# Second mixer of a fused three-layer block: low halves of weights and modulation products taken off GpSimd and put on VectorE in whole tiles

## The chip, the cores and the metric

The kernel runs on one core of one Trainium2 chip. The metric is the device time of one execution in microseconds (us), the median of several runs. The engines are named as in the profile: PE is TensorE (matmuls), PEld its weight loads, DVE is VectorE, ACT is ScalarE, POOL is GpSimd, and SP is SyncE, which issues the DMAs.

## The reference

Three layers are computed in turn over 256 tokens of width 1024. The first is a block with two sparse attentions, the second a block with differential attention (`diff_mixer`), the third a block with a gated delta rule and an axial attention. The change lies in the second layer's mixer, whose reference is:

```
ada = c_act @ ada_w[l] + ada_b[l]
sh1, sc1, g1, sh2, sc2, g2 = jnp.split(ada, 6, axis=-1)
h = modulate(x, sh1, sc1)
q, k, v = jnp.split(h @ w_in, 3, axis=-1)           # 8 heads, each with two 64-wide maps
logits = jnp.einsum('bqhmd,bshmd->bhmqs', qq, k) * scale + bias
p = masked_softmax(logits, dist >= 0)
pd = p[:, :, 0] - lam_full * p[:, :, 1]
o = jnp.einsum('bhqs,bshe->bqhe', pd.astype(v.dtype), v)
o = rms_norm(o, subln) * (1.0 - lambda_init)
y = o @ w_out
```

The modulation vectors (`ada`, six of 1024 values for each of the first two layers) come from a matrix of 1024 x 6144 times one vector.

## The kernel before

**Weights in two halves.** Every weight tile is 128x1024 in float32 (512 KB). It is loaded into a buffer `raw`, ACT rounds it to `hi` (line 347), and the remainder `lo = raw - hi` is a subtraction of two tiles in SBUF (line 352), on DVE or on POOL. Each product is then three matmuls: hi x hi, lo x hi, hi x lo (lines 387 to 389).

**Modulation vectors.** A vector is eight tiles of `ada_w`, each multiplied by the activated conditioning row (`cact`, repeated in all partitions) and summed along its row. `ada_dot` does this for one tile in one of two ways: one DVE instruction that multiplies and sums (line 478, printed as `CUSTOM_DVE_ANT_0` and followed by a short read of the accumulator), or two products of half tiles on POOL (line 461) and a sum on ACT (line 474).

**The second mixer** (`mix1`) works through a list: eight tiles of the value projection (v0 to v7), then q and k of each of the eight heads, one tile of 24 matmuls each, then the output projection. `weave` takes this list one tile at a time and between pieces advances the chains: the eight heads (`queue1`, `head1`), the modulation vectors (1, 3) and (1, 4) (`weave_ada`), and a small preparation for the third layer (`meta_prep`). In this stage the order of instructions on ACT, DVE and POOL is that of the code (`MAN[1]` is `ADG`); the order on PE is left to the scheduler, which sets it when the kernel is built. DMAs are issued by SP in the order of the code, into a ring of seven `raw` buffers, so a load goes out when the tile seven loads earlier has been used.

**Whose low halves.** `SHARE1 = 6`: of the tiles that `weave` prepares here, the first six get a whole `lo` on DVE, the other 20 half on DVE and half on POOL:

```
if share is not None and n > share:
    self.cast_lo(x, nc.vector, 0)
    self.cast_lo(x, nc.gpsimd, 1)
else:
    self.cast_lo(x, nc.vector)
```

**One head** (`head1`): its scores are four matmuls (line 401) into PSUM tiles `y` and `c`; DVE adds the bias and takes the row minimum (line 1625, four instructions); ACT takes the exponentials with row sums (`exps`, line 1658); DVE inverts the sums and scales two of them (lines 1633 and 1634, `drs`); POOL multiplies the second map by them (line 1636, two instructions); DVE combines the two maps (line 1639, two instructions); PE transposes the result (line 1643, `tr<-p_first,se`); ACT copies it (line 1645); PE multiplies it with the values (line 392, into `d`). After every second head `pair1` normalises: squares on ACT (line 1670, `dof`), scalars on DVE (1673), a power on POOL (1674), the product on DVE (1676), transposes on PE (1680), and the split into halves on ACT and DVE (1682, 1684). ACT also copies each q and k out of PSUM (line 1586, `f<-y`); there are two PSUM banks for them.

The eight heads are numbered 0 to 7 in the text.

Of the kernel before, what the change touches and what calls it, by code (L numbers as in the profile page):

```python
# [29 lines left out]
ADA0 = 16  # L30
# [1 line left out]
ADA1 = 17  # L32
ORDER1 = """v0 v1 v2 v3 v4 v5 v6 v7 q0 k0 q1 k1 q2 k2 q3 k3 q4 k4 q5 k5 q6 k6 q7 k7"""
MORE1 = 2
SHARE1 = 6
SHARE0 = None
SHARE2 = 8
MAN = ['A', 'ADG', 'AD', 'ADG', 'P']
# [228 lines left out]
class Kern:  # L267
# [768 lines left out]
    def layer0(self, stop):  # L1036
        nc, ph = self.nc, self.ph
        st = self.st = SimpleNamespace(tok=False, cmp=0, sel=0, lat=False, pc=False, scored=0)
        self.F, self.part, self.oh, self.L0 = {}, {}, None, None
        self.blk = self.T(self.acts, (128, 16, 64), "ol")  # L1040
        nc.gpsimd.memset(self.blk, 0.0)
        self.blkw = self.T(self.acts, (128, 16, 128), "oh", F32R)
        self.tok = self.T(ph, (128, 2, 416), "tok")
        self.hs = self.T(ph, (128, 256), "isc", bufs=3)
        work = []
        for n in ORDER0.split():
            f = (lambda wh, wl, i=int(n[-1]): self.tok0(i, wh, wl)) if n[:3] == "tok" else \
                (lambda wh, wl, n=n[4], i=int(n[5]): self.cmp0(n, i, wh, wl)) if n[:3] == "cmp" else \
                (lambda wh, wl, n=n: self.fm0(n, wh, wl))
            work.append((n if n[:3] == "cmp" else f"ev_{n}", None, f))  # L1050

        def begin(half):
            return half == 0 or st.scored == 4

        self.merged = set()
        work += self.out_work("ev_out", range(4), lambda k: (self.oh[:, k, :], self.ol[:, k, :]),
                              self.merged.__contains__, range(4, 4 + MORE0), begin)
        units = [self.nsa0(j) for j in range(4)] + [self.dsa0(i) for i in range(4)]
        chains = [self.loads0(), self.tok0_after(), self.compress0(), self.compressed0(), self.latent0(), self.queue(units),
                  *(self.merge0(j) for j in range(8)), self.select0(), self.weave_ada((0, 2), (0, 4), (0, 3), start=ADA0)]  # L1060
        self.weave(work, chains, share=SHARE0)
        self.in_order = False
        if stop == "attn0":
            for j in range(8):
                t = self.T(ph, (128, 256), "dbgo", bufs=1)
                nc.vector.tensor_add(t, self.oh[:, j, :].bitcast(F32), self.ol[:, j, :].bitcast(F32))
                self.dump(f"oT{j}", t)
        return stop != "attn0"

    def weave_ada(self, *lvs, start):  # L1070

        nc = self.nc
        for _ in range(start):
            yield
        for lv in lvs:
            t = self.T(self.modp, (128, 8), "mod%d%d" % lv, bufs=1)
            d = self.T(self.small, (128, 8), "adas", bufs=2)
            for m in range(0, 8, 2):
                rest = self.ada_dot(*lv, m, d[:, m:m + 1], "half")
                yield  # L1080
                rest(1)
                yield
                rest()
                self.ada_dot(*lv, m + 1, d[:, m + 1:m + 2], False)
                yield
                yield
            nc.vector.tensor_add(t, d, self.adac[:, 6 * lv[0] + lv[1], :])
            self.mod[lv] = t

# [442 lines left out]
    def mix1(self, stop):  # L1532
# [19 lines left out]
        self.in_order = True  # L1552
        self.weave(work + out, chains, share=SHARE1, man=1)
        self.in_order = False
# [1199 lines left out]
```

## Time and profile before

| | |
|---|---|
| median of 3 runs | 1178.69 us (1178.2 to 1180.43) |
| the profiled execution | 1184.45 us, of which the trace spans 1182.7 us |
| mean granted PE clock of the profiled execution | 0.942 of full speed |
| busy over the span | PE 92%, PEld 84%, DVE 71%, ACT 51%, POOL 27% |
| second mixer, 419 to 547 us | PE busy 115.97 of 128 us, DVE 89.06, ACT 76.91, POOL 70.34 |

The busy time is a sum of each engine's instructions; register, branch, semaphore and DMA-issuing instructions are not counted. The granted clock is the share of full speed that PE's throttle gave; it has two levels, 0.5 (1.2 GHz) and 1 (2.4 GHz). In a row of the timeline the time in brackets is what the engine sat idle before the instruction, and behind the arrow stands what ended that.

### The profile page before, as it was taken

The numbers are of one execution on the slowest core, as the hardware profiler recorded it, in microseconds if no ns is written. First come the engines' busy times: TensorE is split into PE (matmuls) and PEld (weight loads), VectorE is DVE, ScalarE is ACT, GpSimd is POOL, SyncE is SP. The second block draws the span as 40 slices with busy tenths as digits, with TensorE's granted clock in tenths as the row PEclk, the third lists the DMA queues.
The fourth block names the chain that finished last, engine by engine and source line by source line (L and its number), as shares of the span: only waits on it lengthen the run. The fifth ranks groups of instructions, "written<-read, shape, count | busy, mean of one in ns | idle before, by whom it ended". The sixth has DMA issues, their size and how long they took to land.

```text
span 1182.7 us, 20550 instructions
## 1 busy us (share of the span) xinstructions
PE 1088.2 (92%) x7766; PEld 989.8 (84%) x7766; DVE 836.4 (71%) x1656; ACT 603.8 (51%) x1256; POOL 313.5 (27%) x343
## 2 busy tenths in 40 slices
PE   2889989999999999887999999998799989999997
PEld 1768667999999978777999999897786888899996
DVE  7575986799886577766886555579996667755553
ACT  2455757464445456554654444467445353644442
POOL 3283563200000208665000000417654350000000
PEclk9786998999999989898899999899999997999999
DMA  9966642299996238446387554022211151756520
GB/s 344 313 253 208 250 166 82 104 388 345 340 334 230 90 114 279 146 159 232 118 309 251 189 185 140 12 86 93 73 54 37 72 193 45 267 191 184 190 90 36
DMA packets 60448, 212.59 MB, mean 180 GB/s; under 512 B 6619, under 2 KB 9084, under 8 KB 60348
## 3 DMA queue, kind: packets, MB, share of 16 engines
q1 hardware_dynamic: 59424, 209.43, 50.9%
q0 software_dynamic: 192, 0.79, 0.4%
q8 instruction: 61, 1.00, 0.4%
q10 hardware_dynamic: 732, 1.05, 0.3%
q14 instruction: 39, 0.32, 0.1%
HBM read 209.15 MB, written 1.84 MB: 178 GB/s over the span
## 4 chain that ended last, share of the span: by engine, by line
PE 69%; DVE 13%; DMA 5%; POOL 5%; issue 4%; ACT 3%; SPq 0%; POOLq 0%; DVEq 0%; ACTq 0%
PE y L387 10%; PE y L388 10%; PE y L389 10%; PE pj L387 7%; PE pj L388 7%; PE pj L389 7%; PE tr L392 3%; DMA raw<-in_ws 3%; PE y L401 2%; DVE lo L352 2%; PE y L392 1%; PE pj L392 1%; DVE cva L2176 1%; PE cm L392 1%; DVE raw L478 1%
## 5 line engine op out<-in xcount | busy, mean ns | idle before, releaser
L366 DVE TENSOR_TENSOR lo<-raw,hi 128x1024 fp32r<-128x1024 f32 (+1 forms) x208 | 226.8, 1106 | 107.0 <-ACT hi L365 106.9
L365 ACT ACTIVATE hi<-raw 128x1024 fp32r<-128x1024 f32 (+1 forms) x208 | 195.3, 958 | 94.7 <-PE pj L388 77.0
L387 PE MATMUL pj<-hh,hi 128*128 128x256 f32 x768 | 217.1, 283 | 0.3
L388 PE MATMUL pj<-hl,hi 128*128 128x256 f32 x768 | 216.6, 282 | 0.3 <-DVE hl L1749 0.3
L389 PE MATMUL pj<-hh,lo 128*128 128x256 f32 x768 | 215.7, 281 | 0.0
L352 POOL TENSOR_TENSOR lo<-raw,hi 128x512 fp32r<-128x512 f32 (+3 forms) x48 | 75.4, 1577 | 360.6 <-ACT hi L347 355.1
L352 DVE TENSOR_TENSOR lo<-raw,hi 128x1024 fp32r<-128x1024 f32 (+2 forms) x103 | 124.0, 1211 | 41.8 <-ACT hi L347 40.5
L387 PEld LDWEIGHTS pj<-hh,hi 128*128 128x128 f32 x768 | 145.1, 189 | 2.7 <-ACT relu L807 0.9
L388 PEld LDWEIGHTS pj<-hl,hi 128*128 128x128 f32 x768 | 145.1, 189 | 2.0 <-DVE hl L1749 0.5
L388 PE MATMUL y<-actl,hi 128*128 128x256 f32 x512 | 144.3, 282 | 1.3 <-DVE actl L810 1.2
L389 PEld LDWEIGHTS pj<-hh,lo 128*128 128x128 f32 x768 | 145.3, 189 | 0.0
L387 PE MATMUL y<-acth,hi 128*128 128x256 f32 x512 | 144.1, 281 | 0.0
L389 PE MATMUL y<-acth,lo 128*128 128x256 f32 x512 | 143.7, 281 | 0.0
L347 ACT ACTIVATE hi<-raw 128x1024 fp32r<-128x1024 f32 (+2 forms) x107 | 110.7, 1042 | 24.1 <-DMA raw<-in_ws 13.7
L388 PEld LDWEIGHTS y<-actl,hi 128*128 128x128 f32 x512 | 97.0, 189 | 1.9 <-DVE actl L810 1.9
L387 PEld LDWEIGHTS y<-acth,hi 128*128 128x128 f32 x512 | 97.1, 190 | 0.1
L389 PEld LDWEIGHTS y<-acth,lo 128*128 128x128 f32 x512 | 96.8, 189 | 0.0
L478 DVE CUSTOM_DVE_ANT_0 raw<-raw,cact 128x1024 f32<-128x1024 f32 x67 | 86.6, 1301 | 3.3 <-DMA raw<-in_ws 3.1
L388 PE MATMUL y<-hl,hi 128*128 128x256 f32 x296 | 86.6, 293 | 0.0
L387 PE MATMUL y<-hh,hi 128*128 128x256 f32 x264 | 81.5, 309 | 2.2 <-ACT f L1586 2.2
L809 ACT ACTIVATE acth<-act 128x256 fp32r<-128x256 f32 x96 | 39.4, 416 | 83.5 <-DVE act L808 83.5
L389 PE MATMUL y<-hh,lo 128*128 128x256 f32 x264 | 77.9, 295 | 0.0
(658 smaller groups left out, 2556.9 us busy)
## 6 DMA issues: line engine op xcount, KB each, us to landing
raw<-in_ws SPq DMA_DIRECT2D x372, 512.0 KB, 4.7
bm<-bscr SPq DMA_DIRECT2D x4, 512.0 KB, 14.2
raw<-in_ws SPq DMA_DIRECT2D x4, 416.0 KB, 8.8
bm<-in_ws SPq DMA_DIRECT2D x3, 512.0 KB, 8.5
raw<-in_ws SPq DMA_DIRECT2D x3, 408.0 KB, 3.8
zn<-in_ws SPq DMA_DIRECT2D x2, 512.0 KB, 6.9
xa<-in_xT SPq DMA_DIRECT2D x2, 512.0 KB, 6.9
oh<-in_ws SPq DMA_DIRECT2D x2, 512.0 KB, 7.8
```

Source lines behind the costliest of these rows:

```text
L347: return self.nc.scalar.activation(w[1], w[0], AF.Copy)
L352: return eng.tensor_tensor(w[2][:, a:b], w[0][:, a:b], w[1][:, a:b].bitcast(F32), op=OP.subtract)
L365: i = nc.scalar.activation(hi[:, a:b], raw[:, a:b], AF.Copy)
L366: j = (lo_by or nc.vector).tensor_tensor(lo[:, a:b], raw[:, a:b], hi[:, a:b].bitcast(F32), op=OP.subtract)
L387: mm(out, lh, rh, start=start, stop=False, skip_group_check=True)
L388: mm(out, lh, rl, start=False, stop=False, skip_group_check=True)
L389: mm(out, ll, rh, start=False, stop=stop, skip_group_check=True)
L392: self.nc.tensor.matmul(out, l, r, start=start, stop=stop, skip_group_check=True)
L401: last = self.nc.tensor.matmul(out, l, r, start=start, stop=stop, skip_group_check=True)
L478: nc.vector.tensor_tensor_reduce(out=raw, in0=raw, in1=self.cact, op0=OP.mult, op1=OP.add, scale=0.5, scalar=0.0, accum_out=t)
L809: nc.scalar.activation(ah, f, AF.Copy)
L2176: nc.vector.scalar_tensor_tensor(a, x[:, i:i + 272], w[:, j, i:i + 1], a, op0=OP.mult, op1=OP.add)
```

## The change

`SHARE1` becomes `None`, so all low halves of the second mixer are made on DVE in whole tiles. `weave_ada` gets a list `spread` of the vectors that go the way with half products on POOL; the first mixer passes all of its three vectors, the second none, so that the second mixer's two vectors are 16 whole-tile instructions on DVE. The first mixer's instructions stay as they were.

```
-SHARE1 = 6
+SHARE1 = None
...
-                  *(self.merge0(j) for j in range(8)), self.select0(), self.weave_ada((0, 2), (0, 4), (0, 3), start=ADA0)]
+                  *(self.merge0(j) for j in range(8)), self.select0(), self.weave_ada((0, 2), (0, 4), (0, 3), start=ADA0, spread=((0, 2), (0, 4), (0, 3)))]
...
-    def weave_ada(self, *lvs, start):
+    def weave_ada(self, *lvs, start, spread=()):
...
-            for m in range(0, 8, 2):
-                rest = self.ada_dot(*lv, m, d[:, m:m + 1], "half")
-                yield
-                rest(1)
-                yield
-                rest()
-                self.ada_dot(*lv, m + 1, d[:, m + 1:m + 2], False)
-                yield
-                yield
+            for m in range(8):
+                if lv in spread and m % 2 == 0:
+                    rest = self.ada_dot(*lv, m, d[:, m:m + 1], "half")
+                    yield
+                    rest(1)
+                    yield
+                    rest()
+                else:
+                    self.ada_dot(*lv, m, d[:, m:m + 1], False)
+                    yield
+                    yield
```

Over the program this takes 36 instructions from POOL (20 low halves and 16 half products) and eight sums from ACT, makes 20 half subtractions on DVE whole, and gives DVE eight more products with their accumulator reads. Every DMA stays in its place in SP's order. Lines behind the edit have numbers that are larger by two in the changed kernel.

DVE in head 0, from behind the row minima (lines 1625 and 1627) to the combination of the two maps; `lo`, `raw` and `hi` are weight tiles, `se` the two maps. Before:

```order
L352 TENSOR_TENSOR lo_993_5096<-raw_991_5093,hi_992_5095 128x512
L1633 RECIPROCAL drs_5111<-drs_5111 128x4
L1634 TENSOR_SCALAR drs_5111<-drs_5111,nlam_2345 128x2
L478 ISA raw_1010_5175,adas_5034<-raw_1010_5175,cact_87 128x1024
L478 ISA adas_5034 128x1
L352 TENSOR_TENSOR lo_1008_5155<-raw_1006_5152,hi_1007_5154 128x512
L1639 SCALAR_TENSOR_TENSOR se_5118<-se_5118,drs_5111,se_5123 128x128
```

The same place in the changed kernel:

```order
L478 ISA raw_1004_5124,adas_5034<-raw_1004_5124,cact_87 128x1024
L478 ISA adas_5034 128x1
L352 TENSOR_TENSOR lo_993_5092<-raw_991_5089,hi_992_5091 128x1024
L1635 RECIPROCAL drs_5107<-drs_5107 128x4
L1636 TENSOR_SCALAR drs_5107<-drs_5107,nlam_2345 128x2
L478 ISA raw_1010_5168,adas_5034<-raw_1010_5168,cact_87 128x1024
L478 ISA adas_5034 128x1
L352 TENSOR_TENSOR lo_1008_5149<-raw_1006_5146,hi_1007_5148 128x1024
L1641 SCALAR_TENSOR_TENSOR se_5114<-se_5114,drs_5107,se_5119 128x128
```

A product of a whole tile now stands ahead of the reciprocal too, and both subtractions are whole.

POOL between the maps of head 0 (`se_5123`) and head 1 (`se_5232`), before:

```order
L1636 TENSOR_SCALAR se_5123<-se_5123,drs_5111 128x256
L352 TENSOR_TENSOR lo_1008_5155<-raw_1006_5152,hi_1007_5154 128x512
L461 TENSOR_TENSOR raw_1027_5237<-raw_1027_5237,cact_87 128x512
L352 TENSOR_TENSOR lo_1014_5199<-raw_1012_5196,hi_1013_5198 128x512
L461 TENSOR_TENSOR raw_1027_5237<-raw_1027_5237,cact_87 128x512
L1636 TENSOR_SCALAR se_5232<-se_5232,drs_5220 128x128
```

In the changed kernel the four between the two heads are gone, and head 1's scaling follows head 0's directly.

PE from the scores of head 3 (`f,f`) over the transposes of the first pair of heads' normalised output (`dof`) and of head 2's maps (`se`); `y_1069` and `y_1069_5433` are the projection of a k tile, woven in by the scheduler, and `hfull` the meta tokens of the third layer. Before:

```order
L387 MATMUL y_1069_5449<-hh_118,hi_1037_5311 128x256
L401 MATMUL c_5475<-f_5442,f_5390 128x128
L401 MATMUL y_1075_5476<-f_5442,f_5390 128x128
L1680 MATMUL tr_5462<-p_first_89,dof_5370 128x128 x4
L1643 MATMUL tr_5468<-p_first_89,se_5340 128x128 x3
L401 MATMUL c_5475<-f_5442,f_5390 128x256
L401 MATMUL y_1075_5476<-f_5442,f_5390 128x256
L1740 MATMUL tr_5491<-p_first_89,hfull_4971 128x16 x8
```

After:

```order
L401 MATMUL c_5459<-f_5426,f_5376 128x128
L401 MATMUL y_1075_5460<-f_5426,f_5376 128x128
L401 MATMUL c_5459<-f_5426,f_5376 128x256
L401 MATMUL y_1075_5460<-f_5426,f_5376 128x256
L387 MATMUL y_1069_5433<-hh_118,hi_1037_5299 128x256
L388 MATMUL y_1069_5433<-hl_119,hi_1037_5299 128x256
L389 MATMUL y_1069_5433<-hh_118,lo_1038_5300 128x256
L1682 MATMUL tr_5446<-p_first_89,dof_5357 128x128 x4
L1645 MATMUL tr_5452<-p_first_89,se_5328 128x128 x3
```

All four scores of head 3 now stand ahead of the transposes, and three projection matmuls between them. Head 1's, 4's, 5's, 6's and 7's scores (or most of them) have moved ahead of the transposes of the head before in the same way; head 2's have not.

## Rows read from the trace of the kernel before

**Rows 1.** Windows cut where the granted clock (PEclk) changes; stretch, length, busy time by engine.

```profile
474.90:478.30 3.40, 3.40 (x19) 3.04 (x17) 3.40 (x3) 2.34 (x5) 3.40 (x4) 0.52 0.36 136
478.30:481.70 3.40, 0.16 (x2) 0.00 (x0) 3.40 (x2) 0.00 (x0) 2.36 (x2) 0.98 0.05 18
481.70:488.50 6.80, 6.54 (x32) 5.55 (x33) 5.02 (x19) 4.29 (x13) 0.37 (x1) 0.51 0.54 165
522.70:526.10 3.40, 3.40 (x17) 3.40 (x18) 0.11 (x1) 0.00 (x0) 1.26 (x1) 0.52 0.17 69
```

**Rows 2.** Waits of PE from 441 to 547 us: total, times, longest.

```profile
PE tr L1680 <- DVE dof L1676: 3.5, 1, 3.5
PE tr L1643 <- DVE se L1639: 3.2, 4, 1.1
PE y L389 <- POOL lo L352: 2.2, 1, 2.2
PE y L387 <- ACT f L1586: 2.2, 2, 1.8
PE y L389 <- DVE lo L352: 0.9, 1, 0.9
```

**Rows 3.** DVE's timeline in head 1: start, length, what, idle before.

```profile
458.83 0.29 DVE L1625 CUSTOM_DVE_ANT_0 sx<-y,bm 128x128 f32<-128x128 f32 x1 [1.38 <-PE c L401]
...
459.95 1.67 DVE L352 TENSOR_TENSOR lo<-raw,hi 128x512 fp32r<-128x512 f32 x1
...
463.02 0.69 DVE L352 TENSOR_TENSOR lo<-raw,hi 128x512 fp32r<-128x512 f32 x1
463.90 1.99 DVE L1639 SCALAR_TENSOR_TENSOR se<-se,drs,se 128x128 f32<-128x128 f32 x2 [0.19 <-POOL se L1636]
```

**Rows 4.** POOL's timeline from 462 to 481 us.

```profile
462.14 2.18 POOL L1636 TENSOR_SCALAR se<-se,drs 128x128 f32<-128x128 f32 x2 [1.07 <-DVE drs L1634]
464.29 1.32 POOL L352 TENSOR_TENSOR lo<-raw,hi 128x512 fp32r<-128x512 f32 x1
...
473.07 0.82 POOL L1636 TENSOR_SCALAR se<-se,drs 128x128 f32<-128x128 f32 x2 [1.08 <-ACT tr L1730]
474.27 1.47 POOL L1734 TENSOR_TENSOR mss<-mss,mhalf 16x1 f32<-16x1 f32 x1 [0.37 <-DVE mss L1733]
475.72 1.28 POOL L352 TENSOR_TENSOR lo<-raw,hi 128x512 fp32r<-128x512 f32 x1
...
479.41 1.25 POOL L461 TENSOR_TENSOR raw<-raw,cact 128x512 f32<-128x512 f32 x1
```

**Rows 5.** DVE's timeline from 475 to 483 us.

```profile
475.26 5.95 DVE L352 TENSOR_TENSOR lo<-raw,hi 128x512 fp32r<-128x512 f32 x1
481.13 0.68 DVE L1676 TENSOR_TENSOR dof<-d,dr 128x512 f32<-128x512 f32 x1
481.73 0.73 DVE L1639 SCALAR_TENSOR_TENSOR se<-se,drs,se 128x128 f32<-128x128 f32 x2
```

**Rows 6.** Timeline of all engines from 519.5 to 523 us.

```profile
519.84 0.69 DVE L352 TENSOR_TENSOR lo<-raw,hi 128x512 fp32r<-128x512 f32 x1
...
521.11 2.85 POOL L352 TENSOR_TENSOR lo<-raw,hi 128x512 fp32r<-128x512 f32 x2
...
522.58 0.40 PE L389 MATMUL y<-oh,lo 128*128 128x256 f32 x1 [2.25 <-POOL lo L352]
```

**Rows 7.** DVE groups from 441 to 547 us: count, busy, mean ns, idle before.

```profile
L352 DVE TENSOR_TENSOR lo<-raw,hi 128x512 fp32r<-128x512 f32 x20 | 24.1, 1207 | 1.0 <-ACT hi L347 1.0
L478 DVE CUSTOM_DVE_ANT_0 raw<-raw,cact 128x1024 f32<-128x1024 f32 x8 | 10.3, 1291 | 0.4 <-DMA raw<-in_ws 0.4
```

**Rows 8.** DVE groups from 419 to 441 us.

```profile
L352 DVE TENSOR_TENSOR lo<-raw,hi 128x1024 fp32r<-128x1024 f32 x6 | 7.2, 1223 | 3.3 <-ACT hi L347 2.0 <-issue 1.2
```

**Rows 9.** POOL groups from 441 to 547 us.

```profile
L352 POOL TENSOR_TENSOR lo<-raw,hi 128x512 fp32r<-128x512 f32 x20 | 27.7, 1390 | 4.3 <-ACT hi L347 4.3
L461 POOL TENSOR_TENSOR raw<-raw,cact 128x512 f32<-128x512 f32 x16 | 23.2, 1453 | 26.5 <-DMA raw<-in_ws 26.5
```

## The prediction

> **What bounds the kernel now.** I read the busy shares first: PE is busy 92% of the span, so only a place where PE waits or runs slowly can give time back. The edit touches the stage from 419 to 547 us alone; the orders of all engines ahead of it are unchanged, and behind it only a few matmuls have changed places. So I read that stage: first the waits of PE, then the windows of the granted clock, then the timelines of DVE and POOL at the long waits.
>
> PE waits 12.0 us in five groups [rows 2]: 3.5 for the normalised output, 3.2 in four pieces for the combined maps, 2.2 for a low half from POOL, 2.2 for copies by ACT, 0.9 for a low half from DVE. In three stretches it runs at the lower level of its clock, 1.2 GHz, each begun in or just after one of the three longest idle times, 1.8, 3.5 and 2.2 us: 3.4 us from 474.9, 6.8 from 481.7, 3.4 from 522.7 [rows 1]. At a granted 0.52, 0.51 and 0.52 the busy time there loses 3.40 x 0.48 = 1.6, 6.54 x 0.49 = 3.2 and 1.6 us. Together 12.0 + 6.4 = 18.4 us could be had here at most.
>
> The timelines say why PE waits. A half subtraction of 128x512 on DVE takes 0.69 us when POOL is not working on tiles, but 1.67 at 459.95 and 5.95 at 475.26 [rows 3, 5]. In the last case POOL runs four tile instructions back to back, from 475.72 to 480.66 [rows 4]; DVE ends 0.5 us behind them. The reader is to see two engines that exclude each other, not two that each run a little slower: the combination of the maps takes 1.99 at 463.90, while POOL's low half lies at 464.29 to 465.61, and 0.73 at 481.73 with POOL idle [rows 3 to 5]. The other way round, POOL's scaling takes 2.18 from 462.14, until DVE's product and half subtraction have ended (463.71), and 0.82 at 473.07 [rows 3, 4].
>
> **The change part by part.** *Taken from POOL:* 20 low halves (27.7 us) and 16 half products (23.2) [rows 9]. Only the scaling and the small powers are left there in this stage. ACT loses eight sums; it is not waited for at the places below except at 474, where the copy that PE waits for stands behind squares, exponentials and the meta tokens' squares, all of which stay.
>
> *Added to DVE:* eight products at 1.29 = 10.3 us, and 20 whole subtractions in place of half ones. A whole one takes 1.22 where POOL is little used [rows 8], so 20 x 1.22 = 24.5 against the 24.1 that the halves took [rows 7]: doubled work in the same time. Bounds for a whole one: 1.22, and twice the mean half, 2 x 1.21 = 2.41. I take 1.22, since the halves show 0.69 where nothing blocks them, and what blocked them is what goes.
>
> *The chain of a head*, from the first row minimum to the end of the combination, is 465.89 - 458.83 = 7.06 us in head 1 [rows 3]: minima 1.12, low half 1.67, scalars and product 1.40, low half 0.69, POOL's end 0.19, combination 1.99. In the changed order it has one product more ahead of the reciprocal: 1.12 + 1.29 + 1.22 + 1.40 + 1.22 + 0.19 + 0.73 = 7.17. So a head's chain stays as it is: relief and new work cancel, 0.1 us a head, and since instructions overlap by about that at their ends I take zero. If the combination stays at 1.99, the chain is 1.26 longer.
>
> *The long wait at 478.* The subtraction of 5.95 us stood ahead of the product of the normalised output (481.13), for which PE waited 3.5 us at 478.5, with the next 6.8 us slow [rows 1, 2, 5]. With the four POOL instructions gone, product, whole subtraction (1.22), normalised output (0.68) and combination (0.73) end near 474.1 + 1.2 + 0.5 + 1.22 + 0.68 + 0.73 = 478.4, the 0.5 for the power at 474.27 that may still come between. PE now has the four scores of head 3 and three matmuls to do first, which brings it to 479. The wait goes, and the slow stretch behind it: -3.5 - 3.2 = -6.7 us. Bounds: 0 for the clock's part if another idle time follows, and all 6.7.
>
> *The wait at 520.3.* PE waits 2.25 us for a low half that POOL begins at 521.11, behind its scaling; DVE's half of the same tile begins at 519.84 [rows 6]. Whole on DVE it ends at 519.84 + 1.22 = 521.06, so 0.73 of the wait stays: -1.5, and the slow 3.4 us behind it go, -1.6. Together -3.1. Bounds: nothing, if the chain ahead on DVE runs later by 1.5, and -3.9.
>
> *The four short waits (3.2 us).* At three of them the next head's scores now stand ahead of the transposes, so PE has work while it waits. The chain itself stays. I take -1.1 (about 0.35 at each of three); bounds 0 and -3.2.
>
> *What gets worse.* The wait of 0.9 for DVE's half at 530 now is for a whole one, 1.22 - 0.69 = +0.5. Also, the power for every second head and the metaT product on DVE, which now waits for transposes that stand later on PE, can cost some tenths; DVE has gaps there. Every product on DVE now waits for its load in order, with the row minima queued behind it. DVE waited 0.4 us for loads in the whole stage [rows 7]; SP's order is as before, and each new product frees its buffer after one instruction in place of three. I cost this at nothing; the cover is the seven buffers.
>
> *What stays:* 1.8 of the 2.2 us for ACT at 474, and the slow 3.4 us behind it.
>
> **Row and rule.** The low half at 475.26 waited out four POOL instructions, not one [rows 4, 5], and POOL's scaling at 462.14 waited out two of DVE's. The Trainium skill (SBUF — State Buffer, section Who interferes with whom) says that a DVE instruction with two inputs in SBUF and a GpSimd instruction that reads SBUF exclude each other, and that whoever issues first holds the shared ports for the whole instruction. By an instruction-wise hold the scaling would get in between product and low half; the trace shows a run of them held through. By the row the scaling ends 0.19 behind DVE's run, as summed above. With the hold handed over at each instruction DVE's low half would begin later by the scaling's first part, about half of 0.82, and the second part would wait behind it: the chain is longer by 0.2 us a head, 8 x 0.2 = 1.6 in all.
>
> **The sum.** -6.7 - 3.1 - 1.1 + 0.5 = -10.4 us. The profiled execution took 1184.45 (1182.7 of span and 1.75 around it), so 1174.0 by its own measure; it lies 5.8 above the median, in parts I can't place and which the edit doesn't touch. Taken from the median: 1178.69 - 10.4 = **1168.3 us**, 0.9% less. About 0.2% (2.4 us) is what a measurement of this kernel can tell from no change.
>
> **The rivals.**
> 1. *The clock does not come back.* DVE's chains run close to PE's pace, so PE idles elsewhere, for 1.8 us or more, and slow stretches of the same length return. Then 3.2 + 1.6 of the gain are missing: -5.6, 1173.1 us. For it: the idle of 1.8 at 474 was enough. Against: the waits of 1.1 and below were not followed by one.
> 2. *Hold by instruction* (above): -10.4 + 1.6 = -8.8, 1169.9.
> 3. *More goes:* all short waits and the one at 474 with its slow stretch too: up to 18.4, 1160.3. Against: squares and exponentials stand ahead of that copy in both orders.
> 4. *No change:* the combination keeps its 1.99 us because POOL's own second scaling overlaps it. 8 x 1.26 = 10.1 us come back, 1178.4. Against: the 0.73 at 481.73 is the same instruction pair.
> 5. *Slower: the relief does not come.* The product (1.29) and two half subtractions (2 x 0.53) go into each head's chain, ahead of the combination, and the blocked times stay, because what delays DVE is not POOL's tiles. The chain is longer by 2.35 a head, 8 x 2.35 = 18.8, less the 10.4: 1187.1 us. It decides from 1.3 us a head on (10.4 / 8). For it: the order shows all three ahead of the combination. Against: 0.69 and 1.67, or 0.73 and 1.99, for the same work in the same stage, as POOL is free or not.
>
> **How the numbers follow.** My forecast 0.62 (1164 to 1172, its short waits and the wait at 520 between their bounds), clock 0.16, hold by instruction 0.06, more 0.03, no change 0.06, slower 0.07. The range of 1162 to 1176 leaves out the last three, 0.16. Faster by over 0.2%: 0.62 + 0.16 + 0.06 + 0.03 = 0.87; within it 0.06; slower 0.07.
>
> **What will show it.** In the changed kernel's profile: whole low halves on DVE near 1.22 us in the second mixer, with none beyond 2; combinations at 0.7 to 1 us in place of up to 1.99; no wait of PE for the normalised output near 478, and the 6.8 us slow stretch gone; at 520 a wait below 1 us, on DVE in place of POOL, and no slow stretch behind it; the stage shorter by about 10 us. I am wrong if a head's chain from row minimum to combination has grown beyond 8.4 us, if DVE waits for loads, or if PE has new idle times of about 2 us that each bring a slow stretch.

## The result, and the profile after

| | median of runs | ratio to the kernel before, 95% interval |
|---|---|---|
| kernel before | 1178.45 us (1176.76 to 1180.43) | |
| changed kernel | 1165.86 us (1162.97 to 1170.08) | 0.9893 [0.9871, 0.9914] |

12.6 us or 1.1% faster, where 10.4 us were forecast. Times below are medians of 4 to 12 runs, each ratio against the kernel before on the same chip.

I count the stage from the first matmul of the value projection to the first matmul behind it on `eps`: 125.99 us before (418.76 to 544.75), 114.28 after (412.49 to 526.77), 11.7 less. Windows of the changed kernel (stretch, length, busy time of PE, PEld, DVE, ACT, POOL, granted clock, DMA share, GB/s): the only stretch at the lower clock level that begins within the stage, then the whole stage, then what lies ahead and behind:

```profile
468.50:471.90 3.40, 3.40 (x19) 2.78 (x18) 3.40 (x7) 1.72 (x3) 1.26 (x1) 0.52 0.37 122
412.49:526.77 114.28, 110.52 (x786) 98.32 (x785) 88.58 (x211) 66.86 (x177) 23.18 (x21) 0.98 0.55 194
0.00:412.00 412.00, 366.38 (x2683) 329.10 (x2684) 318.49 (x645) 214.02 (x434) 120.90 (x136) 0.94 0.69 247
527.00:1161.00 634.00, 595.48 (x4297) 547.54 (x4296) 432.91 (x816) 313.87 (x630) 125.24 (x150) 0.96 0.41 139
```

The same cuts in the trace of the kernel before:

```profile
418.76:544.75 125.99, 113.96 (x787) 101.89 (x786) 87.97 (x195) 75.59 (x193) 70.08 (x57) 0.94 0.52 176
0.00:418.00 418.00, 374.57 (x2682) 336.48 (x2683) 314.35 (x645) 213.89 (x434) 118.35 (x136) 0.92 0.68 244
545.00:1182.00 637.00, 598.70 (x4297) 551.00 (x4296) 433.36 (x816) 313.51 (x630) 125.08 (x150) 0.96 0.41 139
```

PE's busy time in the stage fell by 3.4 us for the same matmuls, its idle time (length less busy time) from 12.03 to 3.76: -3.4 - 8.3 = -11.7. POOL went from 70.1 us to 23.2, DVE from 88.0 only to 88.6, with eight products and 20 half subtractions more to do. Ahead of the stage all orders are the same, yet the traced execution of before needs 6 us more there, 8.2 us more busy time for the same matmuls at a lower granted clock; so the two traces differ by 21.5 us of span where the medians differ by 12.6.

PE's waits in the changed kernel from 434 us to the end of the stage (total, times, longest), against [rows 2]:

```profile
PE y L387 <- ACT f L1588: 2.2, 2, 1.8
PE tr L1645 <- DVE se L1641: 1.5, 3, 1.0
```

The waits for the normalised output (3.5), for the half from POOL (2.2) and for the half from DVE (0.9) are gone; the one for ACT's copies stands as it was. DVE and POOL groups of the same stretch, against [rows 7, 9]:

```profile
L352 DVE TENSOR_TENSOR lo<-raw,hi 128x1024 fp32r<-128x1024 f32 x20 | 24.4, 1219 | 0.9 <-ACT hi L347 0.8
L478 DVE CUSTOM_DVE_ANT_0 raw<-raw,cact 128x1024 f32<-128x1024 f32 x16 | 19.5, 1218 | 0.0
L1638 POOL TENSOR_SCALAR se<-se,drs 128x128 f32<-128x128 f32 x8 | 14.0, 1753 | 67.2 <-DMA raw<-in_ws 38.8 <-DVE drs L1636 22.1 <-DVE bcol L663 5.3
```

DVE's timeline in head 1 and at the place of the old long wait, against [rows 3, 5]:

```profile
452.21 0.29 DVE L1627 CUSTOM_DVE_ANT_0 sx<-y,bm 128x128 f32<-128x128 f32 x1 [0.65 <-PE y L401]
...
456.39 1.22 DVE L478 CUSTOM_DVE_ANT_0 raw<-raw,cact 128x1024 f32<-128x1024 f32 x1
457.54 1.22 DVE L352 TENSOR_TENSOR lo<-raw,hi 128x1024 fp32r<-128x1024 f32 x1
458.95 0.95 DVE L1641 SCALAR_TENSOR_TENSOR se<-se,drs,se 128x128 f32<-128x128 f32 x2 [0.19 <-POOL se L1638]
...
469.28 1.21 DVE L352 TENSOR_TENSOR lo<-raw,hi 128x1024 fp32r<-128x1024 f32 x1
470.41 0.67 DVE L1678 TENSOR_TENSOR dof<-d,dr 128x512 f32<-128x512 f32 x1
471.01 0.73 DVE L1641 SCALAR_TENSOR_TENSOR se<-se,drs,se 128x128 f32<-128x128 f32 x2
```

POOL's scaling in the same two heads, against [rows 4]:

```profile
456.65 2.72 POOL L1638 TENSOR_SCALAR se<-se,drs 128x128 f32<-128x128 f32 x2 [5.62 <-DVE drs L1636]
...
467.09 0.82 POOL L1638 TENSOR_SCALAR se<-se,drs 128x128 f32<-128x128 f32 x2 [0.92 <-ACT tr L1732]
```

Each low half takes 1.22 us. In head 1 POOL's scaling waits out DVE's product and subtraction together (2.72), and the combination follows 0.19 behind the subtraction; with DVE idle the same scaling takes 0.82. A head's chain is 452.21 to 459.90, 7.69 us.

### The profile page after: what moved, and what is told of

It is laid out like the page before. It is cut to its first block, busy times and chain, and to the rows that moved or that the text cites. A ratio compares the mean times of both kernels' runs of the same rounds, so it can differ in the third digit from the quotient of the medians.

```text
span 1161.2 us, 20465 instructions
## 1 busy us (share of the span) xinstructions
PE 1073.1 (92%) x7766; PEld 975.4 (84%) x7766; DVE 840.5 (72%) x1672; ACT 595.3 (51%) x1240; POOL 269.3 (23%) x307
## 4 chain that ended last, share of the span: by engine, by line
PE 68%; DVE 14%; DMA 5%; POOL 5%; issue 4%; ACT 3%; POOLq 0%; DVEq 0%; ACTq 0%; SPq 0%
PE y L387 10%; PE y L388 10%; PE y L389 10%; PE pj L387 7%; PE pj L389 7%; PE pj L388 7%; DMA raw<-in_ws 3%; PE tr L392 2%; DVE lo L352 2%; PE y L401 2%; DVE raw L478 1%; PE y L392 1%; PE pj L392 1%; DVE cva L2178 1%; POOL se L1457 1%
## 5 line engine op out<-in xcount | busy, mean ns | idle before, releaser
L352 DVE TENSOR_TENSOR lo<-raw,hi 128x1024 fp32r<-128x1024 f32 (+2 forms) x103 | 126.6, 1236 | 42.2 <-ACT hi L347 40.8
L352 POOL TENSOR_TENSOR lo<-raw,hi 128x512 fp32r<-128x512 f32 (+3 forms) x28 | 47.5, 1703 | 357.9 <-ACT hi L347 335.9
L478 DVE CUSTOM_DVE_ANT_0 raw<-raw,cact 128x1024 f32<-128x1024 f32 x75 | 97.1, 1303 | 2.7 <-DMA raw<-in_ws 2.7
```

What stands on the lines that cost most here:

```text
L352: return eng.tensor_tensor(w[2][:, a:b], w[0][:, a:b], w[1][:, a:b].bitcast(F32), op=OP.subtract)
L478: nc.vector.tensor_tensor_reduce(out=raw, in0=raw, in1=self.cact, op0=OP.mult, op1=OP.add, scale=0.5, scalar=0.0, accum_out=t)
```

## The experiments

**Theories.** A: DVE and POOL exclude each other while both read tiles in SBUF, and what went is POOL's reading. B: the gain comes from PE's new order, which puts scores ahead of transposes. C: it comes from ACT's eight sums that are gone. The stage, PE's listed waits in it and the length of the low-clock stretches that begin in it, by trace, in us:

| kernel | median | ratio, 95% interval | stage | PE waits | low clock |
|---|---|---|---|---|---|
| before | | 1 | 125.99 | 12.0 | 13.6 |
| changed | 1165.86 | 0.9893 [0.9871, 0.9914] | 114.28 | 3.7 | 3.4 |
| changed, again | 1165.05 | 0.9886 [0.9844, 0.9928] | 114.74 | 4.5 | 3.4 |
| low halves alone | 1174.40 | 0.9969 [0.9949, 0.9988] | 120.30 | 7.4 | 3.4 |
| products alone | 1173.12 | 0.9955 [0.9933, 0.9976] | 120.51 | 9.5 | 6.8 |
| POOL reads put back | 1181.50 | 1.0026 [1.0003, 1.0050] | 127.58 | 12.6 | 10.2 |
| POOL only writes | 1166.00 | 0.9904 [0.9876, 0.9933] | 114.29 | 3.7 | 3.4 |
| before, POOL only writes | 1162.61 | 0.9878 [0.9855, 0.9901] | 110.69 | 3.9 | 0 |
| no products | 1161.60 | 0.9865 [0.9836, 0.9893] | 109.50 | 2.2 | 0 |
| meta squares earlier | 1169.48 | 0.9936 [0.9915, 0.9957] | 111.27 | 2.1 | 0 |
| the same again | 1170.15 | 0.9936 [0.9909, 0.9963] | 111.28 | 2.1 | 0 |
| third layer too | 1160.10 | 0.9866 [0.9834, 0.9899] | 113.01 | 3.7 | 0 |
| third layer and meta | 1164.69 | 0.9898 [0.9862, 0.9934] | 112.49 | 2.3 | 3.4 |
| all three mixers | 1156.14 | 0.9811 [0.9775, 0.9848] | 114.49 | 4.2 | 3.4 |

By their traces, PE takes the matmuls of the stage in the order of the changed kernel in "changed, again", "POOL reads put back", "POOL only writes", "third layer too" and "all three mixers", and in that of before in "before, POOL only writes". In the other runs the scheduler gave PE another order, and a difference of their stage holds that too.

**Each half of the change by itself.** The kernel before with `SHARE1 = None` alone, and the changed kernel with `SHARE1 = 6` put back:

```
-SHARE1 = 6
+SHARE1 = None
```

> The low halves alone go to DVE whole; the 16 half products stay on POOL and the eight sums on ACT. Theory A (POOL's and DVE's tile instructions exclude each other, and the gain is what that cost): POOL's run at the long wait shrinks from four tile instructions to two, so about 2.5 of the 5 us of blocking stay, the wait of 3.5 us shrinks to about 1 with or without its slow stretch; the wait of 2.2 us for POOL's low half and its slow stretch (together 3.8) go. About -7 us against the kernel before, 1171. Theory B (the gain comes from the order on PE that the scheduler found for the changed kernel): this kernel has an order of its own, so anything between no change and -12. Theory C (it comes from ACT's eight sums): no change.

```
-SHARE1 = None
+SHARE1 = 6
```

> The products alone go to DVE; POOL keeps 20 half subtractions, ACT loses the eight sums. Theory A: POOL's run at the long wait shrinks to two tile instructions too; POOL's low half at 520 still stands behind its scaling, so that wait of 2.2 us and its slow stretch stay, and DVE has 10 us more work with half of the blocking left. About -3 us against before, 1175.5, with DVE's combinations still up to 2 us. Theory C (ACT's sums): the full -12, 1166.

The low halves alone gave less than expected (3.6 us by the medians, for 7), the products alone more (4.9, for 3). In the stage each gives about half: it is 5.7 us shorter with the low halves alone and 5.5 with the products alone, together 11.2 against 11.7. The medians (3.6 and 4.9 below the 1178.0 of before on that chip, 12.6 for both) would say that the parts do less alone than together, but the intervals are too wide to tell. With the low halves alone 1.1 us of the long wait stay, with the products alone 2.9, since two POOL tile instructions still stand beside the subtraction ahead of the normalised output, which takes 4.04 us (whole) and 3.49 (a half) there. With the products alone, PE's waits for DVE and then the groups of shared halves on DVE and POOL (434 to 533 us):

```profile
PE tr L1645 <- DVE se L1641: 4.4, 6, 1.1
PE tr L1682 <- DVE dof L1678: 2.9, 1, 2.9
```

```profile
L352 DVE TENSOR_TENSOR lo<-raw,hi 128x512 fp32r<-128x512 f32 x20 | 19.6, 982 | 0.8 <-ACT hi L347 0.8
...
L352 POOL TENSOR_TENSOR lo<-raw,hi 128x512 fp32r<-128x512 f32 x20 | 28.4, 1434 | 32.2 <-ACT hi L347 32.2
```

The halves on DVE still take 0.98 us where 0.69 is free, and PE's listed waits for maps are longer than before (4.4 for 3.2). That fits a chain of a head that has become longer and is not yet relieved, but PE's order differs too.

**POOL's load put back, as reads or as writes.** The changed kernel with 36 extra POOL instructions on a spare tile that nothing needs, at the old places; the orders of PE, DVE and ACT are those of the changed kernel. Once they subtract tile from tile:

```
+    def load_pool(self):
+        x = self.spare
+        self.nc.gpsimd.tensor_tensor(x[:, 1], x[:, 0], x[:, 0], op=OP.subtract)
```

> The changed kernel, with 36 subtractions of 128x512 put on POOL at the places of the 36 instructions that were taken away; they read and write a spare tile that nothing else uses and wait for nothing. PE's and DVE's orders are those of the changed kernel, word for word. Theory A: DVE's low halves and combinations are blocked again (combinations near 2 us, low halves of 2.5 us and more) and 6 to 12 us of the gain are lost: 1172 to 1178. Theories B and C: nothing is lost but what POOL's scaling waits behind its own queue (up to 1 us at a head): 1166 to 1169, with DVE's instructions at their free lengths.

and once they only fill it:

```
+    def load_pool(self):
+        self.nc.gpsimd.memset(self.spare, 0.0)
+        self.nc.gpsimd.memset(self.spare[:, 0, :256], 0.0)
```

> As the run with subtractions on POOL, but each is replaced by two memsets of together 1280 columns, about the same time (0.95 and 0.31 us), which only write. PE's and DVE's orders are those of the changed kernel. If the exclusion is about reading SBUF on both engines, DVE runs at its free lengths: 1166 to 1169. If any work of POOL on SBUF blocks DVE's two-input instructions, it comes out as the run with subtractions: 1172 to 1178.

With reads the whole gain is lost and more, 1181.5, with PE's new order and ACT's relief in place: B and C alone give nothing. DVE is busy 107.2 us in the stage with reads and 88.8 with writes, for the same instructions. With writes nothing is lost, at 69.52 us of POOL's time in the stage where before had 70.08. Groups with reads (430 to 538 us, which holds 29 of the 36 places):

```profile
L352 DVE TENSOR_TENSOR lo<-raw,hi 128x1024 fp32r<-128x1024 f32 x22 | 30.9, 1404 | 1.0 <-ACT hi L347 1.0
L478 DVE CUSTOM_DVE_ANT_0 raw<-raw,cact 128x1024 f32<-128x1024 f32 x16 | 22.6, 1412 | 0.3 <-DMA raw<-in_ws 0.3
...
L1098 POOL TENSOR_TENSOR spare<-spare 128x512 f32<-128x512 f32 x29 | 36.0, 1243 | 1.6
```

and with writes (434 to 526 us):

```profile
L352 DVE TENSOR_TENSOR lo<-raw,hi 128x1024 fp32r<-128x1024 f32 x21 | 25.6, 1221 | 1.7 <-ACT hi L347 1.6
L478 DVE CUSTOM_DVE_ANT_0 raw<-raw,cact 128x1024 f32<-128x1024 f32 x16 | 19.5, 1219 | 0.0
...
L1097 POOL MEMSET spare<- 128x1024 f32 x29 | 27.6, 952 | 1.2
...
L1098 POOL MEMSET spare<- 128x256 f32 x29 | 9.5, 327 | 1.7
```

The means hide how uneven this is: with reads, the median subtraction takes 1.22 us and the longest 2.57. The 1.41 us of DVE's product beside reads, and 1.22 beside writes, say the same for the product as for the subtraction. The Trainium skill (SBUF — State Buffer, section Who interferes with whom) states that a DVE instruction with two SBUF inputs contends with a GpSimd instruction that reads SBUF and not with one that only writes it; both traces agree.

**The relief without the rest.** The kernel before, its 36 POOL instructions replaced one for one by fills of the same half tiles; the orders of PE, DVE, ACT and SP are those of before:

```
                 sl = slice(512 * i, 512 * i + 512)
+                if l == 1 and v in (3, 4):
+                    nc.gpsimd.memset(raw[:, sl], 0.0)
+                    return
                 nc.gpsimd.tensor_tensor(raw[:, sl], raw[:, sl], self.cact[:, sl], op=OP.mult)
...
-                        self.cast_lo(x, nc.gpsimd, 1)
+                        if man == 1:
+                            nc.gpsimd.memset(x[2][:, 512:1024].bitcast(F32), 0.0)
+                        else:
+                            self.cast_lo(x, nc.gpsimd, 1)
```

> The kernel before, whose 36 POOL instructions on tiles in the second mixer are replaced one by one by fills of the same half tile with zeros (the second halves of the low halves and half of the products are zero); the orders of PE, DVE, ACT and SP are those of before, line for line, and DVE keeps its half subtractions and its eight products. Theory (POOL's reads are the whole cause, the orders of PE and the whole tiles on DVE give nothing): the waits at 478, 520 and 530 go with two of the three slow stretches, and the time is that of the changed kernel or a little less, 1163 to 1168. Rival 1 (the scores that PE's new order puts ahead of the transposes are needed for the gain): the short waits for the combined maps and the one near 478 stay in part, 1170 to 1174. Rival 2 (ACT's eight sums are needed): the waits for ACT stay or grow, about 1169.

1162.6 us: just below the 1163 to 1168 of the theory, and the whole gain without PE's new order, without ACT's relief and without whole tiles. The two DVE instructions of [rows 5], same order, and a half in head 1:

```profile
453.39 0.69 DVE L352 TENSOR_TENSOR lo<-raw,hi 128x512 fp32r<-128x512 f32 x1
...
467.99 0.67 DVE L352 TENSOR_TENSOR lo<-raw,hi 128x512 fp32r<-128x512 f32 x1
468.60 0.67 DVE L1679 TENSOR_TENSOR dof<-d,dr 128x512 f32<-128x512 f32 x1
```

The 5.95 us subtraction takes 0.67. Of the waits, those at 478, at 530 and for the combined maps are gone, but against the theory 1.3 of the 2.2 us at 520 stay, now for a fill:

```profile
PE y L389 <- POOL lo L1991: 1.3, 1, 1.3
```

It stands behind the scaling in POOL's order, and the scaling, which reads a tile, still waits out DVE's product and half (2.18 us from 501.98). These fills are shorter than the reads they stand for (0.52 us each), so POOL is also less busy here; the run with fills of equal total length above excludes that this is what helps.

**What DVE's added work costs.** The changed kernel without the second mixer's 16 products; their loads stay:

```
+                elif lv not in spread:
+                    if m == 0:
+                        nc.vector.memset(d, 0.0)
+                    nc.sync.dma_start(self.raw(), self.wdram("ada%d%d%d" % (*lv, m))[0])
+                    yield
+                    yield
```

> The changed kernel without the 16 products on DVE in the second mixer: the loads stay, the sums are set to zero, so that the two modulation vectors are their bias alone. Each head's chain on DVE is 1.2 us shorter or more, DVE does 20 us less. Theory (PE bounds the stage, the added work on DVE lies beside matmuls): only the 1.5 us for combined maps can go, 1164 to 1166. Rival (the chains of the heads set the pace, and the added products give back part of the relief): the stage shorter by 4 us or more, below 1162.

1161.6, 4.3 below the changed kernel by the medians, which don't separate the two (the intervals of the ratios overlap), and in the stage 4.8 (114.28 to 109.50). That is the rival's side: more than the 1.5 us of listed waits. PE's idle time fell by 1.4 and its busy time by 3.4 (110.52 to 107.11), part of that the slow stretch that this trace doesn't have. "Third layer too" has the changed kernel's order in the stage and no such stretch either: against it 3.5 us are left (113.01 to 109.50), and 2.0 of busy time, which lies in the transposes of the maps (5.38 to 4.36 us) and the scores (9.05 to 8.10).

But PE's order is not the changed kernel's in this run: some transposes of maps, scores and projection matmuls stand elsewhere. So the price of the products is not shown apart from the order's. The same holds against before with fills only (110.69, with eight products and half subtractions on DVE and PE's old order): the changed kernel's stage is 3.6 us longer, and that of "third layer too" 2.3 (113.01 - 110.69). Added work and new order together give back some 2 to 4 us of a relief that is 15.3 in the stage without them (125.99 - 110.69).

**The wait that stayed.** The meta tokens' squares on ACT, which stand ahead of the copy that PE waits 1.8 us for, one piece earlier:

```
-        for _ in range(18):
+        for _ in range(17):
```

> The changed kernel, with the meta tokens' squares on ACT one piece earlier, so that they no longer stand between head 2's exponentials and the copy of k3 for which PE waits 1.8 us at 468 (the scheduler also moves some matmuls of three projections). Theory: with POOL's tiles gone, this wait by ACT is the last long one, and it alone brings the slow stretch behind it. It falls below 0.5 us (-1.4) and the 3.4 us at the lower clock level go (-1.6): about -3 against the changed kernel, near 1163. Rival (the stage has reached what its chains allow, an idle time of the same size shows up elsewhere): no change, 1165 to 1167.

In the stage this did what the theory said: the wait fell to 0.4, the slow stretch went, 111.27 us and -3.0. But the program took 1169.5, 3.6 more than the changed kernel. So it ran once more, with the changed kernel, unedited, beside it:

> The changed kernel itself once more, so that the three other kernels of this turn have it beside them on the same chip. Expected where it was: 1165.9 us, a ratio of 0.989 to the kernel before, within 0.3% of it.

> The kernel with the meta tokens' squares one piece earlier once more: its second mixer is 3.0 us shorter than the changed kernel's, as expected, but its median was 3.6 us above. The low levels of the clock outside the second mixer add up to 143 us in its trace and to 97 in that of the changed kernel. Theory (the clock outside the stage differs between executions, the time of the whole is not told by the stage alone): beside the changed kernel on the same chip it is level with it or up to 3 us faster. Rival (the changed order makes the program slower behind the stage, every time): 3 us or more slower again.

The rival is right: 1170.15 against 1165.05. The ratio to before is 0.9936 both times, against 0.9893 and 0.9886. Behind the stage, where the orders of all engines are the same, the trace has 645.6 us from the end of the stage (523.63) to the end of the span (1169.2), against 634.4 in both traces of the changed kernel, and 646.0 in the first run of this edit. Windows of the second run behind the stage, the whole and one stretch at the lower level,

```profile
524.00:1169.00 645.00, 605.05 (x4296) 557.09 (x4295) 433.73 (x816) 314.16 (x630) 124.90 (x150) 0.95 0.41 137
754.10:757.50 3.40, 3.40 (x17) 3.40 (x17) 0.00 (x0) 0.19 (x1) 1.80 (x14) 0.52 0.00 0
```

and the wait of PE that the changed kernel doesn't have:

```profile
PE a L387 <- DVE full L1781: 2.2, 1, 2.2
```

It is PE's first matmul into the PSUM tile `a`, and in the built program that matmul has a wait on DVE that it doesn't have in the changed kernel. `full` reads the PSUM tile `tr`; that the edit, by taking `tr` tiles in another sequence, left this `tr` in the bank that `a` gets, is argued from the names and not shown. Another 9.6 us are busy time for the same matmuls (605.05 against 595.48): the stretches at the lower clock level behind the stage add up to 72 us in this trace and 53 in the changed kernel's, and half of the 19 between them is 9.6. One of the added ones follows the new wait, at 754. Two others, at 805 and 857, stand at the same places in the traces of "POOL only writes" (801 and 852) and "no products" (799 and 850), which don't have this edit; what brings them stays open. "POOL only writes", with the same orders behind the stage, needs 639.3 us there. So of the 11.2 us more, the traces tie only the new wait of 2.2 and the stretch behind it to the edit.

**The same edit in the other mixers.** The third layer's shared low halves whole on DVE (11 tiles), alone and with the earlier squares:

```
-SHARE2 = 8
+SHARE2 = None
```

> The changed kernel, with the third layer's shared low halves too made whole on DVE (11 tiles, between 790 and 910 us; the orders of ACT and SP are the same). Theory (what the change took away was the exclusion by runs of POOL tiles next to chains that PE waits for): here POOL's halves stand alone, DVE's halves already take 0.70 us on average, so nothing is relieved, and DVE gets 11 x 0.5 = 5.7 us of work in a stretch where PE waits for DVE some 10 us: no gain, 0 to +4 us, 1166 to 1170. Rival (a whole tile on DVE is better than two halves wherever it stands): -2 us or more, below 1164.

> The changed kernel with the third layer's shared low halves whole on DVE (as in the run of that name) and the meta tokens' squares one piece earlier. Theory (the third layer's halves exclude DVE and POOL too, the waits for xp and yd there fell by 4.5 us): 4 to 6 us faster than the changed kernel, and up to 3 more for the meta tokens, 1157 to 1161. Rival (the earlier squares cost as they seemed to): 1163 to 1165.

My theory for the first, no gain or a loss, did not come true: 1160.1, 5.8 below the changed kernel's first median, though the intervals of the ratios overlap (0.9834 to 0.9899 and 0.9871 to 0.9914) and the size stays open. That DVE's halves took 0.70 us over much of this stretch showed that they were not held; it did not show what POOL's halves cost the rest. PE's listed waits for ACT's `xp` and DVE's `yd` fell there by some 4 us. PE's order in this stretch changed with the edit too, and the two are not separated. PE's waits in that stretch (762 to 960 us), in the changed kernel:

```profile
PE b L387 <- ACT xp L2168: 6.5, 3, 3.5
...
PE a L392 <- DVE yd L2468: 2.9, 1, 2.9
```

and with the third layer's low halves whole:

```profile
PE b L387 <- ACT xp L2168: 3.9, 2, 2.9
...
PE a L392 <- DVE yd L2468: 1.5, 1, 1.5
```

By the medians the earlier squares take 4.6 us of that back, as they did without it. Last, the third layer's edit and no half products on POOL in the first mixer either:

```
-self.weave_ada((0, 2), (0, 4), (0, 3), start=ADA0, spread=((0, 2), (0, 4), (0, 3)))
+self.weave_ada((0, 2), (0, 4), (0, 3), start=ADA0)
```

> The changed kernel with no low halves shared in the third layer and no half products on POOL in the first mixer either, so that POOL reads no weight tile beside DVE in any of the three mixers. Theory (exclusion costs wherever a chain that PE waits for runs on DVE beside POOL's tiles): POOL's 14 half products in the first mixer go (24.5 us at 1.77, lengthened by DVE), low halves there fall from 1.49 us to 1.22, and the 4.4 us that PE waits there for maps from POOL fall by half: another 2 to 4 us below the kernel with the third layer alone, 1156 to 1160. Rival (the first mixer is bound by PE and by DVE's own work, POOL's share is a true relief there): 1162 or more.

1156.14, 1.9% below the kernel before and the best of all kernels here: all six runs (1154.06 to 1157.89) lie below all six of the changed kernel on that chip (1160.04 to 1169.21). The first mixer's whole low halves on DVE and PE's wait for the maps (100 to 260 us), first in the changed kernel's second trace:

```profile
L352 DVE TENSOR_TENSOR lo<-raw,hi 128x1024 fp32r<-128x1024 f32 x20 | 30.4, 1526 | 4.5 <-ACT hi L347 4.5
```

```profile
PE tr L1464 <- POOL se L1457: 5.0, 7, 1.5
```

then with none shared:

```profile
L352 DVE TENSOR_TENSOR lo<-raw,hi 128x1024 fp32r<-128x1024 f32 x19 | 24.5, 1290 | 5.2 <-ACT hi L347 5.2
```

```profile
PE tr L1464 <- POOL se L1457: 2.7, 3, 1.4
```

## Why the prediction was right, point by point

**The cause** was as forecast: exclusion of DVE and POOL on tiles in SBUF. Reads put back on POOL take the gain away, writes don't, and the relief alone in the old order gives all of it.

**The sum.** Forecast -10.4 in the stage, by trace -11.7, by medians -12.6 (10.1 to 15.2). The sum is nearer than its parts, and that is luck: PE's idle time fell by 8.3 where the terms have 5.6, its busy time by 3.4 where they have 4.8.

| term | forecast | by trace |
|---|---|---|
| wait at 478 | -3.5 | -3.5 |
| wait at 520 | -1.5 | -2.2 |
| four short waits | -1.1 | -1.7 |
| DVE's half at 530 | +0.5 | -0.9 |
| ACT's copy at 474 | 0 | 0 |
| clock behind 478 and 520 | -4.8 | -3.4, all that PE's busy time fell |

The first term is right in cause and size: the subtraction, the normalised output and the combination run without a break (469.28 to 471.74), 0.8 us ahead of the transposes on PE at 472.58.

**Two terms went wrong.** The wait at 520, of which 0.73 should have stayed, was summed against PE's old order at this place. In the changed order the scores and both groups of transposes (507.49 to 509.28) stand between PE and the low half that ends at 507.77. The order was there to be read; I had read it at the first place only.

The wait at 530 should have grown by 0.5, by a whole low half in place of a half. I had taken the half itself for what PE waits for, and not read the DVE row ahead of it, an addition of 128x8 that took 1.01 us beside a low half on POOL. The two rows before, and the same addition in the old order with fills only:

```profile
528.31 1.28 POOL L352 TENSOR_TENSOR lo<-raw,hi 128x512 fp32r<-128x512 f32 x1 [4.34 <-ACT hi L347]
528.60 1.01 DVE L1087 TENSOR_TENSOR mod<-adas,p_first 128x8 f32<-128x8 f32 x1
...
509.15 0.16 DVE L1090 TENSOR_TENSOR mod<-adas,p_first 128x8 f32<-128x8 f32 x1
```

There it takes 0.16, as it does in the changed kernel, and PE's wait is gone without any change of order; in "POOL reads put back" it takes 1.01 again and PE waits 0.6. So this wait too was exclusion.

**The clock.** Both forecast stretches are gone. That PE's busy time fell by 3.4, and not by 4.8, does not show that they were over-sized. "Third layer too" has the changed kernel's order in the stage and no slow stretch that begins there: PE is busy 109.1 us, 1.4 less than in the changed kernel, for one stretch that length times lost level puts at 1.6. "Before, POOL only writes" has the order of before and none: 106.7 us, 7.3 less than before, for three that the prediction puts at 6.4. What the prediction had at nothing is that the changed kernel's matmuls take 2.4 us more busy time at the upper level (109.1 for 106.7), nearly all in the transposes of the maps (5.38 for 4.12) and the scores (9.05 for 7.95). Whether DVE's added work or PE's order brings this is not shown.

The step that a wait of 1.8 us brings a slow stretch was no law: the same wait of 1.8 for ACT is followed by one in both traces of the changed kernel, and by none in the runs "no products", "third layer too" and "before, POOL only writes". Nor are short waits safe, as rival 1 had them: in "third layer and meta" a stretch of 3.4 us begins at 461.6, with no wait above 1.0 us in the stage.

**The chain of a head** came out at 7.69 us against 7.17, below the 8.4 named as the bound. Its low halves and products had the lengths forecast (1.22, and 1.22 for 1.29); what is more lies in the row minima, 1.56 us from the first to the product behind them (453.77) in place of 1.12, with 0.35 of it idle for a score from PE.

**The holding by runs** (rival 2) is decided for the row: 2.72 us for POOL's scaling, behind a product and a whole subtraction, with 0.19 to the combination. Rivals 4 and 5 fall with combinations of 0.95 and 0.73. The part of rival 5 that holds is that something is given back, some 2 to 4 us with PE's order in it, but the relief is larger. Its price was summed wrongly: it lets the relief not come and still takes off the 10.4; without that it is 1178.69 + 18.8 = 1197.5.

## What to carry to other kernels

Work shared between DVE and POOL was no sharing here, where DVE's instruction reads two tiles in SBUF and POOL's reads there too: a whole tile on DVE took the 1.22 us that the contended half took. The mean does not tell what it costs. One DVE instruction of 5.95 us ahead of a short one that PE needs made PE wait 3.5 us, and an addition of eight columns, held for 1.01, made it wait 0.9. To find out whether an engine's load or its reading hurts, replace its instructions by fills of the same length. And read an edit's price over the whole program: one that took a wait in its stage from 1.8 us to 0.4 brought a new one of 2.2 behind the stage.

## What was not expected of the hardware

Fills on POOL cost DVE nothing that shows: 88.8 us of busy time in the stage with POOL busy 69.5 us of 114, and 88.6 with POOL busy 23.2. An instruction's size does not protect it: an addition of 128x8 took 1.01 us for 0.16. POOL's scaling, which reads one tile, waits out two DVE instructions in a row: 2.72 us for 0.82 in head 1. The same matmuls behind the stage (4296 and 4297 on record) took 9.6 us more busy time in one kernel than in another with the same orders there, with 19 us more at the lower clock level.
